# Stationary tiles of the feed-forward stages at different offsets modulo 512 bytes

## The chip, the core and the metric
The kernel runs on one core of a Trainium2 chip. The metric is the device time in microseconds of one execution, the median of several runs. The profile is one execution taken by the hardware profiler.

## What is computed
One layer of a decoder trunk on x of 256 tokens by 2048 features, in float32, with weights of some 430 MB read once:
```python
x = x + 0.5 * _swiglu(_rmsnorm(x, ffn1_norm[l]), ffn1_w_gu[l], ffn1_w_down[l])
x = x + _token_mixing(_rmsnorm(x, mix_norm[l]), w_in[l], ...)
x = x + 0.5 * _swiglu(_rmsnorm(x, ffn2_norm[l]), ffn2_w_gu[l], ffn2_w_down[l])
```
where `_swiglu(h, w_gu, w_down)` splits `h @ w_gu` (2048 to 2 x 5632) into gate and up and returns `(silu(gate) * up) @ w_down` (5632 to 2048). The token mixing (one input projection, three attention mixers, gates, an output projection) isn't touched by the change.

## The kernel before
Products are made in a split form: every operand is written as a high part of type fp32r and a low part, the rest, and a product is three matmuls, high by high, high by low and low by high (`products`, lines 159 to 163). The weights are the moving operand: a chunk of two k-tiles of 128 rows by 512 columns is loaded by a DMA of SP's queue into one of five raw tiles, ScalarE writes the high part to one of four hi tiles (line 119) and VectorE the low part to one of four lo tiles (line 120). The activations are the stationary operand, 128 features by 128 tokens: xT holds the transposed, normalised x in both parts, midt the transposed result of gate and up, oT and mT the operands of the mixing stage. Each matmul loads a stationary slice of its own: PEld is that load, PE the matmul.

`stream` goes over a list of such chunks in a fixed order; for each it issues the splits of the chunk three ahead, then the chunk's matmuls, then whatever evacuation belongs to it. Other work (transposes, combinations) runs as generators between the chunks, at fixed places.

In the feed-forward stages most chunks are taken in pairs of output columns (`add_pair`), by a scheme of seven block products in place of eight: four of the seven blocks of a pair use as stationary operand not xT or midt but a combination of their quarters, X5, S2, X3 and S3, and as moving operand combinations of the weights made in four sb tiles. The combinations of xT (sax..., four slices of 128 per part) are made once per stage in `combos_x`, those of midt (sam..., two slices) once per group in `combos_m`. A block of a sax tile is 12 matmuls, of a sam tile 6. In the order of the list a pair has a block on xT (or midt) at its head, X5, S2, then a block on xT, then S3, X3 and the rest on xT, with chunks of the pair before it put between the head's blocks. A stage has ten pairs on xT and six on midt; the first chunks of gate and up and the last group of the down product (`add_chunk`) are plain and use xT and midt alone.

All of a stage's own tiles are allotted in `open_pools`, one after the other from where the persistent tiles end: a shift tile of 32 columns, midt, the eight sa tiles, four sb tiles of 8 KB, and small ones (m, f, s5). Per partition, midt takes 24,576 bytes, a sax tile 4,096 and a sam tile 2,048. The persistent tiles in their order are x_sb, xT, the raw, hi and lo tiles, ident, rows, cols and dump, all of a multiple of 512 bytes; then ssq (32 bytes), mhalf (64), three rstd tiles (8), tables of 1,024, 1,024, 3,072 and 512 bytes, and q12 (48), q8, sink and nsink (32 each), gain (12) and w2 (1,024), each of which begins at a multiple of 32 bytes. The mixing stage's pools take the same space between the two feed-forward stages, and a tile's first writer waits for the last user of what lay there.

Of the kernel before, what the change touches and what calls it, by code (L numbers as in the profile page):

```python
# [9 lines left out]
F32 = mybir.dt.float32  # L10
F32R = mybir.dt.float32r
# [5 lines left out]
T, D, FF = 256, 2048, 5632  # L17
# [5 lines left out]
RAW_BUFS, SPLIT_BUFS = 5, 4  # L23
SPLIT_AHEAD = 3
TABLES_AT = 90
NS, NSM = 4, 2
PACE = 2

# [19 lines left out]
def hybrid_trunk_kernel(ctx, tc, x, ffn1_norm, ffn1_w_gu, ffn1_w_down, mix_norm, w_in, qk_gain, sinks, cmp_pos,  # L48
# [32 lines left out]
    def spawn(gen, phase, gap):  # L81
        chains.append([gen, phase, now[0] + gap])
# [57 lines left out]
    def stream():  # L140
        for i, (_, _, nk, width, mm, before, after, _) in enumerate(subs):
            now[0] = i
            split_upto(i + SPLIT_AHEAD)
            if before:
                before()
            run("pre")
            split_upto(i + SPLIT_AHEAD + 1)
            run("mid")
            mm(his[i % SPLIT_BUFS][:, :nk * width].rearrange("p (k c) -> p k c", k=nk),
               los[i % SPLIT_BUFS][:, :nk * width].rearrange("p (k c) -> p k c", k=nk))  # L150
            if after:
                after()
            run("pe")
        while chains:
            now[0] += 1
            for phase in ("pre", "mid", "pe"):
                run(phase)
# [96 lines left out]
    def add_ffn(norm, w_gu, w_down, done):  # L254
        st = {}
# [3 lines left out]
        def open_pools():  # L259
            st["ctx"] = es = ExitStack()  # L260
            p = es.enter_context(tc.tile_pool(name=f"{norm}_mid", bufs=1, reuse_waits="tile"))
            p.tile([128, 32], F32, name=f"{norm}_shift")
            st["mid"] = p.tile([128, 12, 2, T], F32R, name=f"{norm}_midt")
            for w, ns in (("x", NS), ("m", NSM)):
                st["sa" + w] = {n: p.tile([128, ns, 2, 128], F32R, name=f"{norm}_sa{w}{n}")
                                for n in ("X5", "S2", "X3", "S3")}
            st["sb"] = {n: p.tile([128, NS * 512], F32, name=f"{norm}_sb{n}") for n in ("11", "12", "22", "21")}
            st["m"] = [p.tile([128, 512], F32, name=f"{norm}_m{i}") for i in range(2)]
            st["f"] = [p.tile([128, 512], F32, name=f"{norm}_f{i}") for i in range(2)]
            st["s5"] = p.tile([128, 512], F32, name=f"{norm}_s5")  # L270
            spawn(combos_x(), "mid", 4)
            if norm == "ffn1":
                scratch.extend(f[:, 256 * i:256 * (i + 1)] for f in st["f"] for i in range(2))
# [27 lines left out]
        def combos_x():  # L301

            tmp = [t[:, :128 * NS].rearrange("p (k t) -> p k t", k=NS) for t in (*st["f"], st["s5"], st["sb"]["21"])]
            load_block(0, "11", "12", "22")
            for i in range(4):
                tb, h = divmod(i, 2)
                v = xT.bitcast(F32)[:, NS * h:NS * (h + 1), :, 128 * tb:128 * (tb + 1)]
                DVE.tensor_tensor(tmp[i], v[:, :, 0], v[:, :, 1], op=OP.add)
                if i % 2:
                    yield "mid", 1  # L310
            yield from sums(*tmp, st["sax"], 1, 1)
            load_block(0, "21")
# [178 lines left out]
        for gi, (a, b) in enumerate(groups):  # L491
            for c in range(a, b):
                kt0 = 4 * (c - a)
                up = up_evac(kt0, 1 if c == 10 else 3, c == a and b - a > 2)
                if c == 0:
                    add_chunk(w_gu, 0, KT, 0, 512, part(xT), gate_evac, before=open_pools)
                    add_chunk(w_gu, 0, KT, FF, 512, part(xT), up)
                else:
                    add_pair(w_gu, 0, KT, NS, FF + 512 * c, 512 * c, part(xT), "sax", up, gate_evac)
            for j in range(4):  # L500
                evac = down_evac(j, gi == 3)
                if b - a == 2:
                    add_chunk(w_down, 512 * a, 4 * (b - a), 512 * j, 512, part_of("mid", st), evac,
                              before=late if j == 0 else None)
                elif j % 2:
                    add_pair(w_down, 512 * a, 4 * (b - a), NSM, 512 * j, 512 * (j - 1), part_of("mid", st), "sam",
                             evac, down_evac(j - 1, False))
# [780 lines left out]
    if "mix" in stages:  # L1288
        def build():
            late_rows_in()  # L1290
            tables_in()
            yield "pe", 8
            row_cols(16, 86, 16)
            while not ready_late:
                yield "mid", 1
            yield from build_tables()
        if "ffn1" in stages:
            spawn(build(), "mid", TABLES_AT)
    stream()
# [25 lines left out]
```

## Time and profile before

| what | value |
| --- | --- |
| median of 3 runs | 2142.23 us (2141.78 to 2142.64) |
| profiled execution, its own time | 2141.78 us |
| its span in the profile | 2139.9 us |
| TensorE matmul, busy | 2126.0 us, 99% |
| VectorE, busy | 1570.4 us, 73% |
| ScalarE, busy | 1230.6 us, 58% |
| matmuls | 10105 |

The profile gives each instruction a start and a duration. For TensorE's matmuls the duration runs from the start to the end of the pipeline and so overlaps the next ones: the time that a matmul costs in a row of them is the distance between two starts. In a timeline row the first column is the start in us, the second the duration, then come engine, line, operation and the tiles written and read. The first feed-forward stage takes about the first 700 us, the second about the last 690.

### The profile page before, as it was taken

How to read it: one execution, taken by the hardware profiler on the slowest of the kernel's cores; microseconds unless marked ns; L12 is line 12 of the kernel's file. 1: busy time of each engine (PE TensorE's matmuls, PEld its weight loads, DVE VectorE, ACT ScalarE, POOL GpSimd, SP SyncE). 2: the span in 40 equal slices, each digit the busy share in tenths (PEclk: the TensorE clock that was granted, in tenths of full speed). 3: DMA queues.
4: the chain of work that ended last, by engine and by line, in shares of the span. 5: the costliest groups of instructions: out<-in, count | busy, mean ns of one | idle time of the engine just before them, and what ended most of it. 6: DMA issues, size and time to landing. Idle time of an engine off the chain costs nothing.

```text
span 2139.9 us, 27399 instructions
## 1 busy us (share of the span) xinstructions
PE 2126.0 (99%) x10105; PEld 1798.7 (84%) x10105; DVE 1570.4 (73%) x1982; ACT 1230.6 (58%) x1646; POOL 140.7 (7%) x152
## 2 busy tenths in 40 slices
PE   8999999999999999999999999999999999999999
PEld 7888888888888999998888888888888888888887
DVE  7888887888887676666555554658878887887884
ACT  6665665566564566665555444445665665665563
POOL 0000000000000121000001110100000000000000
PEclk9999999999999999999999999999999999999999
DMA  8888878888885575444456666567879878887974
GB/s 296 234 245 238 269 235 231 280 236 234 239 244 173 167 233 146 124 130 130 136 158 196 187 187 196 184 189 235 270 204 286 251 209 270 239 265 208 282 201 150
DMA packets 235950, 459.45 MB, mean 215 GB/s; under 512 B 13272, under 2 KB 42536, under 8 KB 233256
## 3 DMA queue, kind: packets, MB, share of 16 engines
q1 hardware_dynamic: 217096, 402.65, 57.1%
q0 software_dynamic: 18432, 54.53, 14.7%
q8 instruction: 79, 1.29, 0.2%
q10 hardware_dynamic: 288, 0.52, 0.1%
q14 instruction: 55, 0.45, 0.1%
HBM read 428.29 MB, written 2.10 MB: 201 GB/s over the span
## 4 chain that ended last, share of the span: by engine, by line
PE 94%; DVE 2%; ACT 1%; issue 1%; DMA 1%; POOL 0%; DVEq 0%; ACTq 0%; POOLq 0%
PE main L161 23%; PE main L163 23%; PE main L162 23%; PE misc L163 6%; PE misc L161 6%; PE misc L162 6%; DVE lo L120 1%; PE misc L461 1%; PE misc L924 1%; DMA raw<-in_ffn_w_gu_dram 1%; PE misc L1064 1%; ACT hi L119 1%; PE misc L953 0%; PE misc L1035 0%; PE misc L972 0%
## 5 line engine op out<-in xcount | busy, mean ns | idle before, releaser
L120 DVE TENSOR_TENSOR lo<-raw,hi 128x1024 fp32r<-128x1024 f32 (+3 forms) x577 | 681.5, 1185 | 343.9 <-ACT hi L119 335.0
L119 ACT ACTIVATE hi<-raw 128x1024 fp32r<-128x1024 f32 (+3 forms) x577 | 587.5, 1022 | 360.1 <-PE main L163 294.8
L161 PE MATMUL main<-hi,xT 128*128 128x512 f32 (+2 forms) x1480 | 567.7, 384 | 0.0
L162 PE MATMUL main<-lo,xT 128*128 128x512 f32 (+2 forms) x1480 | 557.0, 376 | 1.8 <-DVE lo L120 1.8
L163 PE MATMUL main<-hi,xT 128*128 128x512 f32 (+2 forms) x1480 | 557.3, 377 | 0.0
L119 ACT ACTIVATE hi<-ffn_sb 128x1024 fp32r<-128x1024 f32 x364 | 383.3, 1059 | 262.5 <-PE main L163 112.2
L120 DVE TENSOR_TENSOR lo<-ffn_sb,hi 128x1024 fp32r<-128x1024 f32 x364 | 438.3, 1222 | 112.7 <-ACT hi L119 109.1
L161 PEld LDWEIGHTS main<-hi,xT 128*128 128x128 f32 x1480 | 278.8, 188 | 46.0 <-issue 2.7
L162 PEld LDWEIGHTS main<-lo,xT 128*128 128x128 f32 x1480 | 278.6, 188 | 45.6 <-DVE lo L120 3.3
L163 PEld LDWEIGHTS main<-hi,xT 128*128 128x128 f32 x1480 | 278.2, 188 | 43.5
L161 PE MATMUL main<-hi,ffn_midt 128*128 128x512 f32 x420 | 164.2, 391 | 0.0
L163 PE MATMUL main<-hi,ffn_midt 128*128 128x512 f32 x420 | 163.5, 389 | 0.0
L162 PE MATMUL main<-lo,ffn_midt 128*128 128x512 f32 x420 | 163.4, 389 | 0.0
L357 DVE TENSOR_TENSOR ffn_sb<-ffn_sb,ffn_sb 128x2048 f32<-128x2048 f32 (+1 forms) x64 | 121.1, 1892 | 2.2
L161 PE MATMUL misc<-hi,xT 128*128 128x512 f32 x296 | 115.2, 389 | 0.0
L163 PE MATMUL misc<-hi,xT 128*128 128x512 f32 x296 | 115.2, 389 | 0.0
L162 PE MATMUL misc<-lo,xT 128*128 128x512 f32 x296 | 115.1, 389 | 0.0
L163 PEld LDWEIGHTS main<-hi,ffn_midt 128*128 128x128 f32 x420 | 78.8, 188 | 16.4
L162 PEld LDWEIGHTS main<-lo,ffn_midt 128*128 128x128 f32 x420 | 78.9, 188 | 16.1
L161 PEld LDWEIGHTS main<-hi,ffn_midt 128*128 128x128 f32 x420 | 78.9, 188 | 16.0
L163 PEld LDWEIGHTS misc<-hi,xT 128*128 128x128 f32 x296 | 55.6, 188 | 11.6
L161 PEld LDWEIGHTS misc<-hi,xT 128*128 128x128 f32 x296 | 55.6, 188 | 11.6
(280 smaller groups left out, 2633.6 us busy)
## 6 DMA issues: line engine op xcount, KB each, us to landing
raw<-in_ffn_w_gu_dram SPq DMA_DIRECT2D x191, 512.0 KB, 7.3
ffn_sb<-in_ffn_w_gu_dram SPq DMA_DIRECT2D x80, 1024.0 KB, 7.0
raw<-in_ffn_w_down_dram SPq DMA_DIRECT2D x128, 512.0 KB, 5.2
raw<-in_w_in_dram SPq DMA_DIRECT2D x96, 512.0 KB, 3.6
raw<-in_w_in_dram SPq DMA_DIRECT2D x88, 384.0 KB, 3.4
ffn_sb<-in_ffn_w_down_dram SPq DMA_DIRECT2D x48, 512.0 KB, 6.4
ffn_sb<-in_ffn_w_gu_dram POOLq DMA_DIRECT2D x20, 1024.0 KB, 9.8
ffn_sb<-ffn_sb POOLq DMA_DIRECT2D x20, 1024.0 KB, 7.9
```

Source lines behind the costliest of these rows:

```text
L119: ACT.activation(hi, raw, AF.Copy)
L120: DVE.tensor_tensor(lo, raw, hi.bitcast(F32), op=OP.subtract)
L161: PE.matmul(o, lhs(0), hi, start=start, stop=False, **kw)
L162: PE.matmul(o, lhs(0), lo, start=False, stop=False, **kw)
L163: PE.matmul(o, lhs(1), hi, start=False, stop=stop, **kw)
L357: DVE.tensor_tensor(block_buf(i, dst), block_buf(i, a), block_buf(i, b), op=OP.add)
L461: PE.transpose(bv[:, k, tb * 128:(tb + 1) * 128], m[tb][:, c0:c0 + 128], ident)
L924: PE.transpose(place[i], sb[:, c0:c0 + 128], ident)
L1064: PE.matmul(O[:, 64 + 64 * w:128 + 64 * w], pt[:, i], st["VC"][:, w, kb, 64 * g:64 * g + 64], start=kb == 0, stop=kb == qb)
```

## The change
The shift tile stays. Before each stationary tile of a feed-forward stage (midt and the eight sa tiles) a filler tile of unused columns is put, so that the tile starts at an offset of its own, modulo 512 bytes, from where it started before; the offsets are in a table, multiples of 32 bytes. Behind the last one a further filler brings the sb tiles back to their place modulo 512. Nothing else changes; xT, the hi and lo tiles and the mixing stage's tiles stay.
```diff
+OFFSETS = {"ffn1": {"midt": 32, "saxX5": 64, "saxS2": 96, "saxX3": 160, "saxS3": 192,
+                    "samX5": 224, "samS2": 256, "samX3": 288, "samS3": 320},
+           "ffn2": {"midt": 352, "saxX5": 384, "saxS2": 416, "saxX3": 448, "saxS3": 480,
+                    "samX5": 0, "samS2": 128, "samX3": 32, "samS3": 64}}
...
             p.tile([128, 32], F32, name=f"{norm}_shift")
-            st["mid"] = p.tile([128, 12, 2, T], F32R, name=f"{norm}_midt")
+            at = [128]
+
+            def stationary(shape, name):
+
+                want = (128 + OFFSETS[norm][name]) % 512
+                if at[0] != want:
+                    p.tile([128, (want - at[0]) % 512 // 4], F32, name=f"{norm}_{name}_shift")
+                    at[0] = want
+                return p.tile(shape, F32R, name=f"{norm}_{name}")
+
+            st["mid"] = stationary([128, 12, 2, T], "midt")
             for w, ns in (("x", NS), ("m", NSM)):
-                st["sa" + w] = {n: p.tile([128, ns, 2, 128], F32R, name=f"{norm}_sa{w}{n}")
-                                for n in ("X5", "S2", "X3", "S3")}
+                st["sa" + w] = {n: stationary([128, ns, 2, 128], f"sa{w}{n}") for n in ("X5", "S2", "X3", "S3")}
+            if at[0] != 128:
+                p.tile([128, (128 - at[0]) % 512 // 4], F32, name=f"{norm}_sb_shift")
             st["sb"] = {n: p.tile([128, NS * 512], F32, name=f"{norm}_sb{n}") for n in ("11", "12", "22", "21")}
```

## Rows read from the trace of the kernel before
**Rows 1.** The page: span, busy time of the engines, the chain by engine.
```profile
span 2139.9 us, 27399 instructions
...
PE 2126.0 (99%) x10105; PEld 1798.7 (84%) x10105; DVE 1570.4 (73%) x1982; ACT 1230.6 (58%) x1646; POOL 140.7 (7%) x152
...
PE 94%; DVE 2%; ACT 1%; issue 1%; DMA 1%; POOL 0%; DVEq 0%; ACTq 0%; POOLq 0%
```

**Rows 2.** Feed-forward windows: length, PE, PEld, DVE, ACT, POOL busy (count), clock, DMA, GB/s.
```profile
250.00:640.00 390.00, 390.00 (x1750) 323.56 (x1749) 327.72 (x315) 239.99 (x260) 22.84 (x22) 1.00 0.83 243
1450.00:1840.00 390.00, 389.68 (x1743) 322.79 (x1743) 327.79 (x321) 238.19 (x262) 22.69 (x21) 1.00 0.83 246
```

**Rows 3.** Timeline of TensorE in the mixing stage, an undisturbed stretch.
```profile
1205.13 0.39 PE L161 MATMUL main<-hi,xT 128*128 128x512 f32 x1
...
1244.80 0.39 PE L162 MATMUL main<-lo,xT 128*128 128x512 f32 x1
```

**Rows 4.** Timeline of TensorE in the first feed-forward stage, two stretches.
```profile
299.79 0.39 PE L161 MATMUL main<-hi,ffn_saxS 128*128 128x512 f32 x1
...
301.83 0.39 PE L161 MATMUL main<-hi,ffn_saxX 128*128 128x512 f32 x1
...
342.63 0.39 PE L162 MATMUL main<-lo,ffn_midt 128*128 128x512 f32 x1
...
362.35 0.39 PE L162 MATMUL misc<-lo,ffn_samS 128*128 128x512 f32 x1
```

**Rows 5.** Timeline of TensorE at the start of the kernel.
```profile
9.02 0.63 PE L162 MATMUL main<-lo,xT 128*128 128x512 f32 x1
...
11.58 0.63 PE L162 MATMUL main<-lo,xT 128*128 128x512 f32 x1
...
12.40 0.39 PE L161 MATMUL main<-hi,xT 128*128 128x512 f32 x1
12.63 0.40 PE L162 MATMUL main<-lo,xT 128*128 128x512 f32 x1
```

**Rows 6.** Timeline of both sides of TensorE (PEld loads the stationary slice).
```profile
302.51 0.39 PE L161 MATMUL main<-hi,ffn_saxX 128*128 128x512 f32 x1
302.51 0.19 PEld L162 LDWEIGHTS main<-lo,ffn_saxX 128*128 128x128 f32 x1
```

**Rows 7.** Window of the whole span: matmuls on midt, saxX, saxS, samX in turn.
```profile
0.00:2139.00 2139.00, 409.27 (x1752) 1.00 0.72 215
...
0.00:2139.00 2139.00, 119.08 (x480) 1.00 0.72 215
...
0.00:2139.00 2139.00, 115.41 (x480) 1.00 0.72 215
...
0.00:2139.00 2139.00, 36.54 (x144) 1.00 0.72 215
```

**Rows 8.** Timeline of TensorE: chunks of 420 and of 384 columns.
```profile
735.77 0.35 PE L161 MATMUL main<-hi,xT 128*128 128x420 f32 x1
...
742.69 0.35 PE L161 MATMUL main<-hi,xT 128*128 128x420 f32 x1
...
748.10 0.33 PE L161 MATMUL main<-hi,xT 128*128 128x384 f32 x1
...
752.09 0.33 PE L163 MATMUL main<-hi,xT 128*128 128x384 f32 x1
```

**Rows 9.** Timeline of TensorE in the mixing stage, after attention matmuls.
```profile
1062.59 0.40 PE L162 MATMUL main<-lo,xT 128*128 128x512 f32 x1
1062.83 0.40 PE L163 MATMUL main<-hi,xT 128*128 128x512 f32 x1
...
1063.53 0.39 PE L163 MATMUL main<-hi,xT 128*128 128x512 f32 x1
1063.75 0.39 PE L161 MATMUL main<-hi,xT 128*128 128x512 f32 x1
...
1064.91 0.39 PE L163 MATMUL main<-hi,xT 128*128 128x512 f32 x1
```

## The prediction
> **What bounds the kernel now.** I read the page first, then the windows of the two feed-forward stages, then the timeline of TensorE row by row. The page says that TensorE's matmuls are busy 99% of the span, and the chain of work that ended last runs through them for 94% [rows 1]. In the two windows that hold most of the feed-forward stages TensorE is busy without a gap at a granted clock of 1.00, the higher of its two levels (2.4 GHz), while VectorE, the next engine, is busy 84% and the transfers 83% [rows 2]. So here the time is a number of matmuls times the spacing from one start to the next, and everything else has room. A change that leaves the number of matmuls alone can act only through the spacing.
>
> The durations of the page (389 ns) can't be used for that, because matmuls overlap; the spacing has to be taken from starts in the timeline. A long undisturbed stretch of 512-column matmuls on xT gives (1244.80 - 1205.13) / 175 = 226.7 ns [rows 3], 176 rows from the first shown to the last. The feed-forward tiles have the same: from 342.63 to 362.35 there are 87 spacings, on ffn_midt and in the end the sam tiles, so 226.7 ns, and from 299.79 to 301.83 nine, so 226.7 ns, on ffn_saxS up to ffn_saxX [rows 4]. Streaming alone would be less. At the start of the kernel, right after the first wait for x, six spacings take 2.56 us, 426.7 ns each, and from 12.40 on they are 0.23 us [rows 5]. 426.7 ns is 512 columns at the lower level, 1.2 GHz, with nothing on top (the level is read from the spacing here); at 2.4 GHz that is 213.3 ns. So 13.3 ns of each spacing, 6%, come from something that appears only when the columns stream at the higher clock. What goes on beside the streaming is the load of the next stationary tile: it starts in the same hundredth of a microsecond as the matmul before it [rows 6]. Both read SBUF, and the change moves the one read against the other.
>
> **How the operands lie now.** From x_sb to dump every tile has a size that is a multiple of 512 bytes per partition, so xT and all hi and lo buffers have the same address modulo 512. After them come small tiles that take 384 bytes modulo 512 in steps of 32, and the 32 columns (128 bytes) of the shift tile bring midt and all sa tiles back to that address. Each stationary slice is 128 columns, 512 bytes. So today every stationary slice of these stages stands at offset 0 against the moving operand. The settled 226.7 ns is the spacing of offset 0.
>
> **The change part by part.** (1) Matmuls whose stationary tile moves: 1752 on midt, 480 on saxX, 480 on saxS, 144 on samX [rows 7], and by the code as many on samS as on samX, in all 3000. One tile keeps offset 0: samX5 of the second stage, 6 pairs of 6 matmuls, 36. So 2964 matmuls get another offset; the matmuls on xT, mT and oT stay as they are.
>
> What a spacing is at another offset the trace hardly shows, since all long runs are at 0. Two neighbours exist.
> First, the chunk of 420 columns: there the second slice of hi and lo starts 1680 bytes after the first, 144 modulo 512, so half of its matmuls read with stationary and moving 144 bytes apart. Its spacing is (742.69 - 735.77) / 36 = 192.2 ns; 420 columns at 2.4 GHz are 175.0, so 17.2 ns on top. The chunk of 384 columns right behind it, where both slices are at offset 0, has (752.09 - 748.10) / 23 = 173.5 ns, and 13.5 on top of 160.0, the same as 512 columns [rows 8]. So a narrower matmul by itself changes nothing, and the chunk with shifted slices pays some 3.8 ns more per matmul.
> Second, the matmuls right after an interruption by attention work: from 1062.59 to 1064.91 ten spacings take 2.32 us, 232.0 ns each, single ones between 0.22 and 0.24 us [rows 9], with the same operands at offset 0. The two read streams there stand in another relation in time, and only after some ten matmuls does the spacing fall to 226.7 and stay there. Most relations between the two streams thus cost 5.3 ns more than the one that offset 0 settles into. Moving the address is another way of changing that relation.
>
> I take the middle of the two, 4.6 ns: neither row is the changed operand itself, and the offsets of the change are spread over all multiples of 32. That gives 2964 x 4.6 ns = 13.6 us. Bounds: nothing in the rows excludes a gain, and the streaming alone would give 213.3, that is -13.3 x 2964 = -39.5 us; the largest spacing of the disturbed stretch, 0.24 us, gives +13.3 x 2964 = +39.5 us.
>
> A page speaks to this. The Trainium skill, "TensorE: Matmul & The Clock Gate", "Step-by-step: what each phase is for", says that TensorE has two independent read ports in SBUF and that loading the next tile's weights doesn't steal SBUF bandwidth from the running matmul; by it the offset can't matter and the sum would be 0 us. The same page, "Wait — 56ns, not 53.3ns?", gives 215.7 ns for 512 columns at the higher clock. The trace disagrees with that figure for these operands: 226.7 ns.
>
> (2) Changes of offset along the way. Today the stream passes from xT to a sa tile and back within one spacing [rows 4]. With different offsets the relation has to settle again. Each of the 20 pairs on xT comes back to xT three times from a combination, and midt gives way to xT about 18 times: some 78 entries to xT, whose own offset is unchanged. After an interruption settling costs at most 10 x 5.3 = 53 ns; I take half, 27 ns, so 2.1 us (bounds 0 and 4.1).
>
> (3) The padding. 512 bytes in the first stage and 1536 in the second; sb, m, f and s5 move by these, and their place modulo 512 is kept by the last shift tile. VectorE and ScalarE write the sa tiles and midt at multiples of 32 bytes instead of 512: 84% busy VectorE [rows 2] hides a few ns per write, and if it did not, the writes, some dozens in a stage, are too few to count in microseconds. In the second stage sb tiles overlap tiles of the mixing stage; sb11 already overlaps mT and its first gate and sb22 then reach 160 bytes into a gate tile that has long been read. SP's load of a block waits for those as now; behind it on SP's queue stand the raw loads, which run several tiles ahead. I cost it at nothing; without that lead it would be once one landing, some 7 us. No instruction, DMA or engine queue is added or reordered.
>
> Sum: 13.6 + 2.1 = 15.7 us on the profiled execution's 2141.78 us (span 2139.9 and 1.9 around it), so 2157.5. The median of the runs is 0.45 above that execution: 2158 us.
>
> **The rivals.**
> (a) It settles again. At any constant offset the two streams may fall into 226.7 after some matmuls, as xT does after an interruption. Then only the changes of tile cost: 7 per pair in the code's order of blocks, 32 pairs, and some 36 between xT and midt, about 260, at 27 ns: 7.0 us, 2149 us. For it: the settling is seen after every interruption. Against it: the combination blocks are only 6 or 12 matmuls long, so most would never settle, and the 420-column chunk doesn't within 37 rows.
> (b) The offset doesn't matter: the two reads don't meet at addresses at all, or the 13.3 ns depend on something that repeats every 32 bytes or less, since all offsets are multiples of 32. Then 2142 us. For it: a stationary slice covers all of 512 bytes whatever its start, so a load that runs beside the moving stream passes every offset once. Against it: the 420-column row, and that the spacing is not 213.3. This is the case in which the change doesn't do what it says. The rule of the Trainium skill named above would put it here.
> (c) Faster. The interference of 13.3 ns is that of offset 0, and other offsets avoid part of it. If half of it goes on all 2964, the gain is 6.65 ns x 2964 = 19.7 us, 2122 us; the whole gives 2103. It decides if the mean spacing over the offsets falls below 226.7: below it by 1.45 ns it is worth the 0.2% (4.3 us) that a measurement of this kernel can tell from no change. VectorE at 84% would not stop it [rows 2]. For it: single spacings of 0.22 us in the disturbed stretch [rows 9]. Against it: of the ten spacings there only one is that low, and their mean is 232.0.
> (d) Far worse. Most offsets at the largest disturbed spacing, 0.24: up to 2182 us.
>
> **How the numbers follow.** The forecast (own range 2151 to 2166: 3.8 x 2964 = 11.3 us with no settling, 5.3 x 2964 + 4.1 = 19.8 us) gets 0.46; (a) 0.17; (b) 0.15; (c) 0.17; (d) 0.05. The likeliest gives 2158. A range of 2134 to 2168 holds the forecast, (a), (b) and the smallest gains of (c), some 0.82. Faster by over 0.2% (below 2137.9): 0.17; within it: 0.17, which is (b) and the low edge of (a); slower: 0.66.
>
> **What would show it.** In the profile after, the spacings on ffn_midt, read from starts as in [rows 4], should be 230 to 232 ns and differ between the two stages (offsets 32 and 352); those on xT deep inside a run stay 226.7, with some larger ones right after a combination block. Spacings of 226.7 at every offset but the first few show (a), everywhere (b). The windows of [rows 2] should hold about 1730 matmuls in 390 us instead of 1750, and the mixing stage should keep its length. If spacings on several offsets are near 216, the forecast is wrong in its sign, and the step that failed is taking disturbed timing as a stand-in for a shifted address.

## The result and the profile after

The changed kernel takes 2160.83 us, median of 3 runs (2160.5 to 2161.37), against 2142.23 before: the ratio is 1.0087 with an interval of 1.0064 to 1.011, so 18.6 us slower. The forecast was 2158, its own range 2151 to 2166.

The page of after, with span, busy times and the chain by engine, answers to [rows 1]:
```profile
span 2159.6 us, 27400 instructions
...
PE 2146.4 (99%) x10105; PEld 1799.5 (83%) x10105; DVE 1572.2 (73%) x1982; ACT 1231.3 (57%) x1646; POOL 140.7 (7%) x152
...
PE 94%; DVE 2%; ACT 1%; issue 1%; DMA 1%; POOL 0%; SPq 0%; ACTq 0%; DVEq 0%; POOLq 0%
```
The span is 19.7 us longer, with the same number of matmuls, the same chain and other engines whose busy times differ by less than 2 us. So no new wait came in. The windows of [rows 2], taken again from after:
```profile
250.00:640.00 390.00, 390.00 (x1721) 318.90 (x1721) 322.44 (x308) 235.57 (x254) 22.84 (x22) 1.00 0.82 241
1450.00:1840.00 390.00, 389.46 (x1721) 318.37 (x1720) 319.42 (x315) 232.35 (x258) 21.81 (x20) 1.00 0.81 242
```
TensorE still fills both windows at the same granted clock of 1.00, but fits 1721 matmuls where 1750 and 1743 stood; the prediction said about 1730. The timeline of TensorE in after shows the spacing on the moved tiles, the counterpart of [rows 3, 4]. In turn: ffn_midt of the first stage (offset 32), xT deep in a run and then ffn_saxX of the second stage (offset 384), and ffn_midt of the second stage (offset 352):
```profile
346.18 0.40 PE L166 MATMUL misc<-hi,ffn_midt 128*128 128x512 f32 x1
...
361.11 0.40 PE L167 MATMUL main<-lo,ffn_midt 128*128 128x512 f32 x1
...
1526.18 0.39 PE L166 MATMUL misc<-hi,xT 128*128 128x512 f32 x1
...
1534.57 0.39 PE L167 MATMUL misc<-lo,xT 128*128 128x512 f32 x1
...
1535.03 0.40 PE L166 MATMUL main<-hi,ffn_saxX 128*128 128x512 f32 x1
...
1537.83 0.40 PE L166 MATMUL main<-hi,xT 128*128 128x512 f32 x1
...
1592.10 0.40 PE L167 MATMUL main<-lo,ffn_midt 128*128 128x512 f32 x1
...
1608.50 0.40 PE L168 MATMUL main<-hi,ffn_midt 128*128 128x512 f32 x1
```
On midt of the first stage 64 spacings take 14.93 us, 233.3 ns each; on xT 37 take 8.39, 226.8, which within the rounding of the rows is the 226.7 of before; on saxX 12 take 2.80, 233.3; on midt of the second stage 70 take 16.40, 234.3. They don't settle to 226.7 in the longest runs: read in single nanoseconds the spacings go round a short cycle, 235, 232, 235, 231 at offset 32 and seven values from 230 to 238 at offset 352.

Summed over the trace, the spacings between 205 and 300 ns hold 1811.1 us in after and 1790.2 before, 20.9 more; all others together are 1.1 us shorter. With each spacing counted for the matmul that it starts at, the moved tiles account for 18.5 us of it (midt 11.8, saxS 2.7, saxX 2.4, samS and samX together 1.5), xT for 2.2.

### The profile page after: what moved, and what is told of

The parts are those of the page before. It is cut to its first block, busy times and chain, and to the rows that moved or that the text cites. A ratio compares the mean times of both kernels' runs of the same rounds, so it can differ in the third digit from the quotient of the medians.

```text
span 2159.6 us, 27400 instructions
## 1 busy us (share of the span) xinstructions
PE 2146.4 (99%) x10105; PEld 1799.5 (83%) x10105; DVE 1572.2 (73%) x1982; ACT 1231.3 (57%) x1646; POOL 140.7 (7%) x152
## 4 chain that ended last, share of the span: by engine, by line
PE 94%; DVE 2%; ACT 1%; issue 1%; DMA 1%; POOL 0%; SPq 0%; ACTq 0%; DVEq 0%; POOLq 0%
PE main L166 23%; PE main L167 23%; PE main L168 23%; PE misc L166 6%; PE misc L167 6%; PE misc L168 6%; PE misc L477 1%; PE misc L940 1%; DVE lo L125 1%; ACT hi L124 1%; DMA raw<-in_ffn_w_gu_dram 1%; PE misc L1080 1%; PE misc L242 0%; PE misc L969 0%; PE misc L1051 0%
## 5 line engine op out<-in xcount | busy, mean ns | idle before, releaser
L124 ACT ACTIVATE hi<-ffn_sb 128x1024 fp32r<-128x1024 f32 x364 | 383.6, 1059 | 269.3 <-PE main L168 121.6
L125 DVE TENSOR_TENSOR lo<-ffn_sb,hi 128x1024 fp32r<-128x1024 f32 x364 | 439.7, 1222 | 121.6 <-ACT hi L124 117.5
L166 PE MATMUL main<-hi,ffn_midt 128*128 128x512 f32 x420 | 167.0, 398 | 0.0
L168 PE MATMUL main<-hi,ffn_midt 128*128 128x512 f32 x420 | 166.2, 396 | 0.0
L166 PEld LDWEIGHTS main<-hi,ffn_midt 128*128 128x128 f32 x420 | 79.0, 188 | 18.5
L168 PEld LDWEIGHTS misc<-hi,xT 128*128 128x128 f32 x296 | 55.6, 188 | 11.8
```

The costliest lines, as they stand in the source:

```text
L124: ACT.activation(hi, raw, AF.Copy)
L125: DVE.tensor_tensor(lo, raw, hi.bitcast(F32), op=OP.subtract)
L166: PE.matmul(o, lhs(0), hi, start=start, stop=False, **kw)
L168: PE.matmul(o, lhs(1), hi, start=False, stop=stop, **kw)
```

## The experiments

**Padding alone.** The kernel before, with 1536 bytes more in the shift tile, so that all the tiles move but none changes its place modulo 512.
```diff
-            p.tile([128, 32], F32, name=f"{norm}_shift")
+            p.tile([128, 32 + 384], F32, name=f"{norm}_shift")
```


> The kernel before with 1536 bytes of unused columns in front of midt in both feed-forward stages: as much padding as the change has at most, and every stationary tile still at offset 0 modulo 512. If the offset modulo 512 is what costs, the time is that of before, 2142 us, and spacings on midt and the sa tiles stay at 226.7 ns. If it is the moved sb tiles or the padding itself, the time is near 2160 us.

Measured: 2141.49 us against 2141.14 of before beside it, ratio 1.0001 (0.9992 to 1.0011). The unused columns cost nothing.

**The moving side moved instead.** In the kernel before, hi and lo start 96 bytes later, and shift tiles keep the stationary tiles where they were. Now every 512-column matmul, on xT, mT and oT too, has the one offset 416 (stationary less moving, modulo 512).
```diff
+    per.tile([128, 24], F32, name="moving_shift")
...
-            p.tile([128, 32], F32, name=f"{norm}_shift")
+            p.tile([128, 8], F32, name=f"{norm}_shift")
```


> The kernel before with the hi and lo tiles moved by 96 bytes and every stationary tile left where it was (the shift tiles are 96 bytes shorter), so that stationary against moving is 416 modulo 512 everywhere, in the mixing stage too, and constant from one tile to the next. If a constant non-zero relative offset costs some 5 to 7 ns per matmul, about 9000 matmuls of 512 columns and 1200 of 384 and 420 columns give 2142 + 10200 x 6 ns = 2203 us (2190 to 2215). If the cost comes from passing between tiles with different offsets, nothing changes: 2142 us. If the place of the stationary tile by itself matters, 2142 us too.

Measured: 2190.33 us, ratio 1.0229 (1.0212 to 1.0247), at the low edge of what was expected. The timeline of TensorE in this kernel, a stretch on xT in the mixing stage without an interruption:
```profile
1218.42 0.40 PE L162 MATMUL main<-hi,xT 128*128 128x512 f32 x1
...
1239.66 0.39 PE L163 MATMUL main<-lo,xT 128*128 128x512 f32 x1
```
91 spacings take 21.24 us, 233.4 ns; over the trace the spacings that lie twelve or more into a run, some 6,800, have a mean of 233.3. Here all stationary tiles share one offset and none was moved, so the cost needs neither a change of offset from tile to tile nor another place of the tile. A constant relative offset does, and it does not wear off: that refutes rival (a).

**Both sides moved.** 160 bytes ahead of x_sb move everything together.
```diff
+    per.tile([128, 40], F32, name="all_shift")
```


> The kernel before with 160 bytes of unused columns ahead of all tiles: every address moves by 160 bytes, moving and stationary alike. If only the relative offset counts, 2142 us and 226.7 ns. If the place modulo 512 by itself counts, the time differs by some 60 us either way.

Measured: 2142.31 us (one run) beside 2141.14, and 226.7 ns on the spacings deep in a run, again some 6,800. Only the relative offset counts.

**A scan of offsets.** The two feed-forward stages alone (the mixing stage is left out); hi and lo are read s columns into longer buffers, another s for each 21 chunks. The stationary tiles have two places there (xT and the others 320 bytes apart), so each s gives two offsets.
```diff
+    def at(t, si, lo):
+        o = SCAN[min(si // 21, len(SCAN) - 1)][lo]
+        return t[si % SPLIT_BUFS][:, o:o + SPLIT_KT * 512]
```


> Only the two feed-forward stages (the mixing stage is left out), with every stationary tile at one offset and the part of the hi and lo tiles in use moved every 21 chunks: in the first stage by 0, 32, 64 ... 480 bytes, in the second by 4, 8, 12, 16, 20, 24, 28, 48, 80, 112, 144, 240, 272, 400, 496 and 508 bytes. Relative theory: each region of 252 matmuls settles to a spacing of its own, 226.7 ns at 0, 233 to 234.5 ns at 160 and 480 bytes (offsets 352 and 32 of the change, where midt has 234 and 233), 229 to 235 ns at the others, none below 226.7; below 32 bytes unknown. If the spacing depends on distinct neighbours alone, all regions settle at 226.7 ns.

Measured, mean spacing in ns without the first twelve after each change (* five spacings only), offsets that differ by 256 side by side:
```
  0 227.1    32 233.4    64 233.3    96 234.2   128 232.8*  160 233.4   192 228.9   224 233.3
256 226.6*  288 233.4   320 233.4   352 234.2   384 233.2   416 233.3   448 228.9   480 233.4
 16 226.7    48 234.6   208 233.4     4 228.2   300 238.7   316 239.3   484 227.5   508 237.1
272 234.8   304 234.6   464 233.4   324 230.0   488 233.3   500 228.9   504 232.5   432 231.1
```
At multiples of 32 the spacing repeats every 256 bytes, not 512; nothing settles below 226.6; and steps below 32 bytes count, up to 239. Rows of its timeline, first ffn_saxS and ffn_saxX at offset 336, then xT at offset 16:
```profile
1320.47 0.39 PE L166 MATMUL main<-hi,ffn_saxS 128*128 128x512 f32 x1
...
1326.07 0.39 PE L166 MATMUL main<-hi,xT 128*128 128x512 f32 x1
...
1329.92 0.39 PE L168 MATMUL misc<-hi,xT 128*128 128x512 f32 x1
```
24 spacings of 233.3 ns, then 17 of 226.5. One pair seems to break the period: 16 has 226.7 and 272 has 234.8. The runs at the two show why a mean misleads there: at 272 a run of 17 spacings settled at 226.7, two at 236.6 and 236.8, one at 233.4; at 16 a long run settled at 226.7, but one of 11 spacings goes round 234 and 239 by turns, the cycle of the 236.6. So an offset can hold more than one cycle, and which one a run falls into isn't set by the offset alone. What came before it may decide; that was not tried by itself.

**Hi and lo at offsets of their own.** The same scan with a different s for hi and lo (feed-forward stages alone).
```diff
-SCAN = [(0, 0), (8, 8), ...
+SCAN = [(0, 8), (0, 16), ..., (0, 64), ..., (16, 80), ...
```


> Only the two feed-forward stages (the mixing stage is left out); hi and lo tiles moved by different amounts, in columns of 4 bytes, hi first: (0,8) (0,16) (0,24) (0,32) (0,40) (0,48) (0,56) (0,4) (8,0) (16,0) (32,0) (48,0) (16,48) (16,32) (48,32) (0,0), then in the second stage (4,4) (64,64) (0,64) (64,0) (0,2) (2,0) (0,12) (4,0) (68,68) (68,4) (0,68) (9,9) (11,11) (13,13) (16,80) (48,112). The scan before showed offsets 256 apart with the same spacing. If the pattern has a period of 256 bytes, (64,64), (0,64) and (64,0) all have 226.7 ns like (0,0), and (16,80) has what 64 bytes had, 233.3. If each load only meets the matmul beside it, (0,x) lies one third and (x,0) two thirds of the way from 226.7 to the spacing at x. A pair below 226.7 would be a way to a faster kernel; I expect none.

Measured: hi at 0 and lo at 256 settle at 226.7 ns, both at 256 at 226.7, hi at 448 with lo at 192 at 228.9: at multiples of 32, two offsets that are equal modulo 256 act as one. Off them it can be otherwise: hi at 48 with lo at 304 has one run at 234.7, the number of 48, and one at 230.1. Unequal pairs lie anywhere between 228.9 (hi 384, lo 0) and 235.6 (hi 0, lo 464); the expected sum of one third and two thirds of the single offsets doesn't give them: hi 0 with lo 480 should have had 228.9 and has 233.3. No pair is below 226.7.

**The other order of reading.** The feed-forward stages alone, with operands read in other orders, so that the products are no longer the layer's: fewer or other columns of the stationary slice, or the 512 moving columns taken alternately from n parts of the tile.
```diff
+            return t.rearrange("p (h c) -> p c h", h=n) if v == "m" else t
...
+        if v == "h":
+            return f[:, s0:s0 + n]
```


> Only the two feed-forward stages, and with products that are not the reference's: in regions of 21 chunks the stationary slice is read with a step of 2 or of 4 columns, or one column 128 times, or only its first 64, 32 or 96 columns; or the moving operand is read in interleaved order (2 to 256 parts). First stage at offset 0, second with hi and lo moved by 128 bytes. If the 13.3 ns come from the weight load's reads meeting the moving reads, they shrink with the columns loaded: about 10 ns at 96, 7 at 64 and 3 at 32 columns, and the order of reading changes them. If they are a fixed cost of changing weights, they are 13.3 ns in all of these.

The timeline of TensorE in this kernel: loads of 32 columns on xT at offset 0; then the moving columns from two halves by turns, on xT, saxS and saxX; then from four parts:
```profile
257.58 0.39 PE L189 MATMUL main<-hi,xT 128*32 128x512 f32 x1
...
261.75 0.39 PE L189 MATMUL misc<-hi,xT 128*32 128x512 f32 x1
...
299.66 0.38 PE L190 MATMUL misc<-lo,xT 128*128 128x512 f32 x1
...
307.65 0.38 PE L191 MATMUL main<-hi,ffn_saxX 128*128 128x512 f32 x1
...
312.62 0.44 PE L189 MATMUL main<-hi,xT 128*128 128x512 f32 x1
...
329.62 0.45 PE L189 MATMUL main<-hi,ffn_midt 128*128 128x512 f32 x1
```
With 32 columns to load 18 spacings take 4.17 us, 231.7 ns, and the tiles at offset 320 have 231.6; with 64 columns it is 230.0 at offset 0 and 232.7 at 320, with 96 columns 230.0 and 228.5. So the cost does not shrink with what the load reads, and the expectation that it would is refuted; it isn't a fixed 13.3 ns either. The order of the load's reads does count: with the moving operand read in a row as before, a stationary slice read with a step of two columns settles at 233.3 ns on xT at offset 0, where the plain slice has 226.7, and at 230.2 at 320; a step of four gives 234.8 at offset 0 and 240 at 384, and one column read 128 times about 231 at each of the offsets 320, 192 and 384. Columns from two halves by turns give 37 spacings in 7.99 us, 215.9 ns, across tiles at offsets 0 and 320 alike; with the moving side 128 bytes on (offsets 384 and 192) it is 215.8 as well. Four parts give 60 spacings in 17.00 us, 283.3 ns; eight have 493, and sixteen to 256 between 431 and 461.

**Multiples of 256.** The changed kernel with midt, S2 and S3 at offset 256 and X5 and X3 at 0. There are still fillers, and neighbouring tiles still differ modulo 512, but every offset is zero modulo 256.
```diff
-OFFSETS = {"ffn1": {"midt": 32, "saxX5": 64, "saxS2": 96, ...
+OFFSETS = {"ffn1": {"midt": 256, "saxX5": 0, "saxS2": 256, ...
```


> The changed kernel with another table: midt, S2 and S3 at 256, X5 and X3 at 0, so that neighbouring tiles still differ modulo 512 and as many tiles are shifted. If the pattern has a period of 256 bytes, as the scan showed for constant offsets, every spacing settles at 226.7 ns and the time is that of before, 2142 us. If differing neighbours cost something, some 150 changes between 0 and 256 at 27 ns give 4 us more, 2146 us; if 512 is the period, 2150 to 2160 us.

Measured: 2141.09 us against 2141.18, ratio 1.0 (0.9991 to 1.0009). The whole 18.6 us hang on the offset modulo 256.

**Reading by turns in the whole kernel, split by turns.** The kernel before; the splits write even columns to the first half of hi and lo and odd ones to the second, and the matmuls read the halves by turns, so the column order comes out as it was. The second run is the same edit on the changed kernel.
```diff
+        raw = raw.rearrange("p (k c h) -> p k h c", k=m, h=2)
+        hi, lo = (t.rearrange("p (k h c) -> p k h c", k=m, h=2) for t in (hi, lo))
...
+            mm(his[i % SPLIT_BUFS][:, :nk * width].rearrange("p (k h c) -> p k c h", k=nk, h=2),
```


> The kernel before, with hi and lo written as two halves (even columns, then odd ones) by a split that reads raw and sb with a step of two columns, and read by the matmuls alternately from the two halves, so that columns come out in their natural order. The probe of reading orders had 215.9 ns per 512 columns there. If the extra spacing belongs to the order in which the moving operand is read, 9000 matmuls of 512 and fewer columns lose 10.8 ns each, 97 us: 2045 us, or up to 30 us more where VectorE (84% busy in the feed-forward stages, 88% then) or the transfers become the limit, or where the strided split takes longer. If the split with a step of two takes a third longer, VectorE is the limit and nothing is gained.

> The same interleaved order in the changed kernel, with its table of offsets. If the interleaved read has no meeting with the weight load left, the offset no longer matters: the same time as the interleaved kernel at offset 0, within 0.2%, and 215.9 ns on all tiles. If the offset still acts, some 15 us more than that.

Measured: 2171.19 us, ratio 1.0137 (1.0122 to 1.0153), and 2169.1, ratio 1.0131 (1.0117 to 1.0144). Both are slower than before, and within 0.1% of each other. That alone says little on the offset, because TensorE is no longer the limit here; the spacings say more, 216 ns in the median on every tile in both. From the first one's page (groups of instructions: busy, mean ns), its window of the first stage and its longest wait of TensorE (us in total, times, longest):
```profile
L122 ACT ACTIVATE hi<-ffn_sb 128x1024 fp32r<-128x1024 f32 x364 | 547.9, 1560 | 138.4 <-DVE ffn_sb L361 94.3
L123 DVE TENSOR_TENSOR lo<-ffn_sb,hi 128x1024 fp32r<-128x1024 f32 x364 | 540.3, 1510 | 42.2 <-ACT hi L122 40.3
```
```profile
250.00:640.00 390.00, 368.13 (x1683) 309.73 (x1683) 361.85 (x301) 311.71 (x249) 21.57 (x20) 1.00 0.80 238
```
```profile
PE main L166 <- DVE lo L123: 37.1, 46, 2.1
```
The splits of 128x1024 took 1059 ns on ScalarE and 1222 on VectorE before; read with a step of two they take 1560 and 1510. VectorE is now busy 93% of the window and TensorE 94%: the matmuls wait for their lo parts, and the gain in spacing is lost. Over the whole span spacings of more than 300 ns between 512-column matmuls hold 112 us beyond 216 ns each, against 12 in the kernel before. A small part is the clock: the granted clock fell to the lower level for some 10 us in all (mean 0.997), which can account for 5 us.

**Blocks in place of single columns.** The feed-forward stages alone, again with products that are not the layer's: the moving operand is read in blocks of 1, 2, 4, ... columns by turns from the two halves, with PSUM written in a row or in the same blocks, and some splits write by turns instead of reading so.
```diff
+    def cut(t, e):
+        return t.rearrange("p (h c e) -> p c h e", h=2, e=e)
```


> Only the two feed-forward stages, products not the reference's where only the reading order is changed. The moving operand is read alternately from its two halves in blocks of 1, 2, 4, 8, 16, 32, 64 and 128 columns, written to PSUM in a row; then in blocks of 2 to 128 with PSUM written in the same blocks, which puts the columns back in their natural order without any change to the splits. First stage at offset 0, second with hi and lo moved by 32 bytes; in the second stage every other region also has a split that reads in a row and writes hi and lo alternately into the halves. Blocks of 1 had 215.9 ns before. If what helps is that successive reads of 4 bytes go to two places, only blocks of 1 (perhaps 2) have it and the others are near 227 to 233. If any break of the run of reads helps, larger blocks have it too. Writing PSUM in blocks costs nothing from blocks of 2 on, or makes the matmuls much slower, as strides of 4 parts did on the reading side. A split that writes alternately takes 1.06 us on ScalarE like the plain one if only strided reading is slow, 1.5 us or more if any stride is.

Measured, median or settled mean in ns, the first stage: blocks of one column 216, two 327, four 250, eight 243, sixteen 240, thirty-two 237, and from 64 on the numbers of a plain read (226.7 on xT, 233.3 on the tiles at 320). Of the orders tried single columns by turns are the only one that helps. Writing PSUM in the same blocks costs nothing more (two 327, four 250 to 252, eight 243). Splits that write by turns mostly take 2.0 to 2.8 us on ScalarE, longer than those that read by turns.

**Reading by turns, order undone later.** Plain splits as before; only the 512-column matmuls read the halves by turns. Their results come out with the two halves of columns interleaved, and that is undone where they are read anyway: the transposes of m and mg take every second column, the additions to x_sb read PSUM with a step of two. The second run is the same on the changed kernel.
```diff
+        if hi.shape[-1] == 512:
+            hi, lo = (t.rearrange("p (h c) -> p c h", h=2) for t in (hi, lo))
...
-                        PE.transpose(bv[:, k, tb * 128:(tb + 1) * 128], m[tb][:, c0:c0 + 128], ident)
+                        PE.transpose(bv[:, k, tb * 128:(tb + 1) * 128], m[tb][:, c0:c0 + 255:2], ident)
...
-                    DVE.scalar_tensor_tensor(xs, bank[tb], 0.5, xs, op0=OP.mult, op1=OP.add)
+                    xs = xs.rearrange("p (h c) -> p h c", h=2)
+                    DVE.scalar_tensor_tensor(xs, bank[tb].rearrange("p (c h) -> p h c", h=2), 0.5, xs, op0=OP.mult,
+                                             op1=OP.add)
```


> The kernel before, with its plain splits; the matmuls of 512 columns read their moving operand alternately, one column from the first half and one from the second, and the order of columns that this gives in PSUM is undone where results leave it: the transposes of m and mg take every second column, and the evacuations into x_sb read PSUM with a step of two. The reading order alone had 215.9 ns in place of 226.7. About 7850 matmuls of 512 columns, 10.8 ns each: 85 us less, 2057 us, if TensorE stays the limit; VectorE then stands at 88% and the transfers at 87% in the feed-forward stages, so up to 25 us of it may be lost in waits: 2057 to 2082 us. If reading PSUM with a step of two, or the transposes, cost what the strided split cost, 2100 us or more.

> The same alternate reading in the changed kernel, with its table of offsets. If the offset acts only through a contiguous read of the moving operand, this is within 0.2% of the alternate kernel at offset 0, and the 18 us of the change are gone. If the offset acts on the weight load whatever the moving order, it is some 15 to 20 us slower than that.

Measured: 2072.0 us against 2141.51, ratio 0.9677 (0.9664 to 0.9691), faster than both kernels; on the changed kernel 2072.39, ratio 0.9678 (0.9665 to 0.9692). The page of the first, a stretch of its timeline over xT, midt and the sam tiles, and its longest wait of TensorE (us in total, times, longest):
```profile
PE 2048.6 (99%) x10105; PEld 1809.7 (87%) x10105; DVE 1566.9 (76%) x1982; ACT 1224.7 (59%) x1646; POOL 141.1 (7%) x152
...
PE 76%; DVE 10%; DMA 6%; issue 5%; ACT 3%; SPq 0%; POOL 0%; ACTq 0%; DVEq 0%; POOLq 0%
```
```profile
299.74 0.38 PE L164 MATMUL misc<-hi,xT 128*128 128x512 f32 x1
...
319.81 0.38 PE L164 MATMUL main<-hi,ffn_midt 128*128 128x512 f32 x1
```
```profile
PE main L165 <- DVE lo L120: 7.5, 15, 1.5
```
93 spacings take 20.07 us, 215.8 ns. Some 7,850 matmuls at 10.8 ns less would be 85 us; the spacings between 205 and 300 ns did fall by 81.8 us (1790.2 to 1708.4), and all others rose by 11.5, together 70.3 of the 70.6 by which the span fell. Some 6 of the 11.5 are waits for lo parts, 7.5 us in 15 waits where the kernel before had 1.8 in 3. The step of two at the evacuation costs nothing that the page shows: the additions to x_sb from PSUM take 682 ns each in both kernels. The chain shows the new bound coming: TensorE has 76% of it instead of 94%, VectorE 10% and the transfers 6%.

## Why the prediction was right, step by step

**What bounds the kernel** was read rightly: with count and clock unchanged, only the spacing moved, and the account of the spacings (20.9 less 1.1) gives 19.8 us, against 19.7 of the span.

**Term (1)**, 2964 matmuls at 4.6 ns, 13.6 us, was mis-sized: it measured 18.5 us, 6.2 ns each. This is the term of the sum that was short, by 4.9 us. The forecast of 2158 missed 2160.83 by less, 2.8, and that is luck: the other spacings came out 1.1 us shorter, which the sum didn't have, and the profiled execution of after stands 0.54 above its median where that of before stood 0.45 below. Both neighbours of the trace were low. The chunk of 420 columns mixes slices at two offsets (the matmuls on either slice stand near 193 ns), so its 3.8 ns are no price of one offset; and the disturbed stretch, 5.3 ns, is a stretch on its way to settling, while a constant offset stays in its cycle. So the sign sought on midt, 230 to 232 ns, was also too low: 233.3 and 234.3. midt carries most of the matmuls, and its offsets 32 and 352 are among the dearer multiples of 32 (6.7 and 7.6 ns above 226.7); the cheaper ones in the table were 192 and 448 (3.1 and 2.2 ns above before), 0 (0.5) and 256 (3.3 here, in blocks of six matmuls that follow a tile at another offset; nothing in the kernel with multiples of 256). The prediction's own range, 2151 to 2166, is wider than the two sums it names for it, which give 2153.5 and 2162; the result lies in both.

**Term (2)**, the entries to xT, 2.1 us, measured 2.2: right. It rests on what the prediction took from [rows 9], that the spacing settles within some ten matmuls. Those rows themselves end after eleven matmuls, but the rest of the trace of the kernel before bears it out, and shows more: in single nanoseconds the runs of 512-column matmuls follow one path, whose spacings are 240, 235, 234, 236, 224, 231, 235, 229, 232, 231, then 226 to 227 for good. [rows 9] is this path from its start; the run from 304.30 us joins it with its second spacing at the third step, that from 341.94 us two steps before its end. All 78 runs of eight spacings or more follow it. So settling costs some 10 to 60 ns, according to where a run joins, and 30 in the mean, near the 27 that the prediction took. **Term (3)**, the padding at nothing, is shown by the first experiment.

**The reason given**, that the load of the next stationary tile and the moving stream meet in SBUF, is borne out only in part. That the relative offset decides, and not the place of either, is shown by moving one side, then both. That the cost comes from how much the load reads is refuted: 32 columns to load cost 230.8 to 231.6 ns at the four offsets tried, where 128 cost 226.7 to 233.4. How the load reads does count, by 6.7 ns for a step of two at offset 0 with the same moving read. How the moving operand is read counts most: by turns from two halves it has 215.8 ns at every offset tried. So both reads have a part in it. What they meet in stays open; no run here leaves the load out, or moves it in time against the stream.

**The rivals.** (a) is refuted: with one constant offset some 6,800 spacings deep in a run have a mean of 233.3. (b) is refuted for this read order and true for the other: read by turns, kernels with and without offsets agree within 0.1%, with TensorE 99% busy in the last pair. (c) was wrong for every offset tried (nothing settled below 226.6), though the 13.3 ns above pure streaming that it counted on can mostly be had, by another read order: 10.8 of them. (d) didn't come: only offsets off the multiples of 32 reach 239 ns. The Trainium skill, "TensorE: Matmul & The Clock Gate", "Wait — 56ns, not 53.3ns?", gives 215.7 ns for 512 columns; the trace has that only with the read by turns, 215.8.

## What to carry to other kernels

Where TensorE is full, read the spacing from starts, compare it with columns over clock, and treat the rest as a cost to be explained: of the 13.3 ns here 10.8 could be had, 3% of the kernel's time. Keep stationary and moving tiles equal modulo 256 bytes if the moving operand is read in a row, and try columns by turns from two halves, with the order undone at a reader for which a step of two costs nothing, as the additions from PSUM here. Before giving an engine a strided read, price it: on the splits it ate more than the matmuls gained.

## What was not expected of the hardware

- The spacing of 512-column matmuls depends on the relative address of its two operands: 226.7 ns at 0 and 256, 228.9 to 234.2 at other multiples of 32 bytes, up to 239.3 between them. At offset 0 it takes one and the same path of at most ten spacings after an interruption before it settles.
- It settles into short cycles of up to seven spacings, and one offset can hold several: 226.7, 233.4 and 236.6 ns were all seen at 272.
- Moving columns by turns from two halves stream at 215.8 ns whatever the offset; from four parts 283, from eight 493, and in blocks of two columns 327.
- A step of two on 128x1024 float32 takes ScalarE from 1059 to 1560 ns and VectorE from 1222 to 1510.
